# The first x tile of an interleaving kernel as one DMA instead of two halves, and the first y tile issued ahead of the opening barrier

## The chip, the cores and the metric

The kernel runs on one core of a Trainium2 chip. The metric is the device time of one execution in microseconds (us), the median of several runs; a separate, profiled execution gives the profile and the trace.

## The reference

Two float32 arrays x and y of shape 32 x 256 x 1024 are interleaved along their last dimension. Nothing is computed; 67.11 MB are read and 67.11 MB written.

```python
result = np.zeros((batch, seq, dim * 2), dtype=np.float32)
result[..., 0::2] = x
result[..., 1::2] = y
```

## The kernel before

Each input is taken as one flat row of numbers and cut into n = 8 tiles of 128 partitions x 8192 float32 (4 MiB; one partition's row is 32 KiB). On the chip there are two buffers for x tiles (xt), two for y tiles (yt) and two for output (ot). An output buffer is also 128 x 8192, and holds one column half of a tile's result: 4096 numbers of x and 4096 of y per partition, alternating.

Three engines share the work, each with its own program, written out in order:

- SP (SyncE) issues the loads, on one DMA queue (q1 in the profile). For tile k it issues x (line 45) and then y (line 48). From k = 2 on it waits first: for x, until three of the four copies of tile k-2 are done, for y until all four are. The counter for that is the semaphore `woven`, which each copy raises by one.
- DVE (VectorE) makes four copies for each tile: for column half h = 0 and then 1, x into the even places of ot[h] (line 60) and y into its odd places (line 63). Ahead of the first copy it waits for the x tile, ahead of the second for the y tile, and from k = 1 on ahead of each half for the store of the same half of the tile before.
- ACT (ScalarE) issues the stores on a second DMA queue (q10), one of 4 MiB for each half, when that half's two copies are done (lines 67 and 68).

TensorE and GpSimd have no part in the work. The 16 DMA engines of the core serve both queues; a DMA of 128 rows gives each of them 8 rows. In the trace each row is one packet, and each engine ends its share of a DMA with a tiny packet that raises the semaphore.

The first x tile is an exception. Lines 37 and 38 load it as two DMAs, columns 0 to 4095 and 4096 to 8191, so with rows of 16 KiB. The second has a semaphore of its own, `hsem`, and DVE waits for it at line 57, ahead of the second half's x copy. The loop over the loads leaves x out for k = 0 (line 44).

After the program is written, `tile_interleave_kernel` moves two instructions by hand. The opening block of the program holds a barrier over all engines, and on SP a drain ahead of it. The loop of lines 89 to 107 runs twice: each time it takes the first DMA of SP that is still in a later block, and puts it in the opening block just ahead of SP's drain.

```python
for engine in (mybir.EngineType.SP, mybir.EngineType.SP):
    ...
    opening.insert(gate, moved)
```

Before the change, the two that are moved are the halves of the first x tile, and y's first DMA is the first one behind the barrier.

Of the kernel before, what the change touches and what calls it, by code (L numbers as in the profile page):

```python
# [3 lines left out]


def _interleave(nc, x, y, out):
    P = 128
    W = 8192
    H = W // 2  # L10

    total = 1
    for s in x.shape:
        total *= s
    n = total // (P * W)
    assert n * P * W == total

    def rows(ap, names, k):
        flat = ap.rearrange("b s d -> (b s d)")
        return flat[k * names : (k + 1) * names].rearrange("(p w) -> p w", p=P)  # L20

    fp32 = mybir.dt.float32
    xt = [nc.alloc_sbuf_tensor(f"xt{b}", [P, W], fp32).ap() for b in (0, 1)]
    yt = [nc.alloc_sbuf_tensor(f"yt{b}", [P, W], fp32).ap() for b in (0, 1)]
    ot = [nc.alloc_sbuf_tensor(f"ot{b}", [P, W], fp32).ap() for b in (0, 1)]

    xsem = [nc.alloc_semaphore(f"xsem{b}") for b in (0, 1)]
    hsem = nc.alloc_semaphore("hsem")
    ysem = [nc.alloc_semaphore(f"ysem{b}") for b in (0, 1)]
    woven = nc.alloc_semaphore("woven")  # L30
    osem = [nc.alloc_semaphore(f"osem{b}") for b in (0, 1)]

    xs = [rows(x, P * W, k) for k in range(n)]
    ys = [rows(y, P * W, k) for k in range(n)]
    os_ = [rows(out, 2 * P * W, k) for k in range(n)]

    nc.sync.dma_start(out=xt[0][:, :H], in_=xs[0][:, :H]).then_inc(xsem[0], 16)
    nc.sync.dma_start(out=xt[0][:, H:], in_=xs[0][:, H:]).then_inc(hsem, 16)

    for k in range(n):  # L40
        b = k % 2
        if k >= 2:
            nc.sync.wait_ge(woven, 4 * (k - 2) + 3)
        if k:
            nc.sync.dma_start(out=xt[b], in_=xs[k]).then_inc(xsem[b], 16)
        if k >= 2:
            nc.sync.wait_ge(woven, 4 * (k - 2) + 4)
        nc.sync.dma_start(out=yt[b], in_=ys[k]).then_inc(ysem[b], 16)

    for k in range(n):  # L50
        b = k % 2
        for h in (0, 1):
            c = slice(h * H, (h + 1) * H)
            if h == 0:
                nc.vector.wait_ge(xsem[b], 16 * (k // 2 + 1))
            elif k == 0:
                nc.vector.wait_ge(hsem, 16)
            if k:
                nc.vector.wait_ge(osem[h], 16 * k)
            nc.vector.tensor_copy(out=ot[h][:, 0::2], in_=xt[b][:, c]).then_inc(woven, 1)  # L60
            if h == 0:
                nc.vector.wait_ge(ysem[b], 16 * (k // 2 + 1))
            nc.vector.tensor_copy(out=ot[h][:, 1::2], in_=yt[b][:, c]).then_inc(woven, 1)  # L63

    for k in range(n):
        for h in (0, 1):
            nc.scalar.wait_ge(woven, 4 * k + 2 * h + 2)
            nc.scalar.dma_start(
                out=os_[k][:, h * W : (h + 1) * W], in_=ot[h]
            ).then_inc(osem[h], 16)  # L70

    nc.scalar.wait_ge(osem[0], 16 * n)
    used = sorted(s.num for s in [*xsem, hsem, *ysem, woven, osem[0]])
    assert used == list(range(used[0], used[-1] + 1)), used
    nc.scalar.sem_clear(range(used[0], used[-1] + 1))
    nc.sync.nop(nofuse=True).wait_op(osem[1], 16 * n, "sem-ge").then_inc(
        osem[1], -16 * n
    )


def kernel(tc, x, y, out):
    nc = tc.nc
    tc.close()
    tc.compile()

    _interleave(nc, x, y, out)

    blocks = nc.main_func.blocks
    for engine in (mybir.EngineType.SP, mybir.EngineType.SP):
        opening = blocks[0].instructions  # L90
        at, moved = next(
            (b, i)
            for b in blocks[1:]
            for i in b.instructions
            if i.engine == engine and i.opcode == "DMACopy"
        )
        assert not (moved.sync_info and moved.sync_info.on_wait)
        body = at.instructions
        body.remove(moved)
        gate = next(  # L100
            n
            for n, i in enumerate(opening)
            if i.engine == engine and i.opcode == "Drain"
        )
        opening.insert(gate, moved)
        at.instructions = body
        blocks[0].instructions = opening


# [1 line left out]
_INS = ['x', 'y']  # L111
_OUTS = [((32, 256, 2048), 'float32')]


# [23 lines left out]
```

## Time and profile before

| | before |
|---|---|
| median of 3 runs | 314.38 us (314.33 to 314.55) |
| profiled execution | 314.29 us |
| its span, first to last instruction | 313.0 us |
| DVE busy | 72.6 us, 32 copies of 2.29 us |
| moved by DMA | 134.22 MB, mean 429 GB/s |
| load DMAs | 17: two of 2048 KB, fifteen of 4096 KB |
| store DMAs | 16 of 4096 KB |

The span is what the trace covers; the profiled execution's own time is 1.29 us longer. The profile doesn't count the issue of a DMA as busy time, so SP and ACT have no row of their own there; their issues are seen in the timeline as SPq and ACTq. A DMA's time to landing runs from its issue and so holds the time in which it stood in the queue behind others.

### The profile page before, as it was taken

To read this page: it belongs to the slowest core of one execution; us is meant where nothing else is said; L and a number is where in the kernel's file an instruction comes from. 1 tells how busy PE (TensorE), PEld (TensorE's weight loads), DVE (VectorE), ACT (ScalarE), POOL (GpSimd) and SP (SyncE) were. 2 spreads that over 40 slices of the span, in tenths; PEclk is the share of its full clock that TensorE was granted. 3 is DMA by queue.
4 is the path that set the end of the run, shared out by engine and by line. 5 is a ranking of instruction groups with operands and counts; after the bars stand their busy time and mean duration, and the time that the engine had idled before them with its cause. 6 is when DMAs were issued, how large, how long until landed. Compare 5 with 4: busy or idle time off the path is not lost.

```text
span 313.0 us, 113 instructions
## 1 busy us (share of the span) xinstructions
DVE 72.6 (23%) x32; POOL 0.2 (0%) x4
## 2 busy tenths in 40 slices
DVE  0226002231022410325003150031501305013510
POOL 0000000000000000000000000000000000000000
DMA  8999999999999999999999999999999999999998
GB/s 341 463 410 394 469 402 448 423 436 436 419 452 406 465 402 469 402 469 402 469 402 448 423 436 436 419 452 406 465 402 469 402 469 402 465 406 444 427 431 373
DMA packets 4752, 134.22 MB, mean 429 GB/s; under 512 B 528, under 2 KB 528, under 8 KB 528
## 3 DMA queue, kind: packets, MB, share of 16 engines
q1 hardware_dynamic: 2448, 67.11, 50.1%
q10 hardware_dynamic: 2304, 67.11, 49.7%
HBM read 67.11 MB, written 67.11 MB: 429 GB/s over the span
## 4 chain that ended last, share of the span: by engine, by line
DMA 82%; DVE 12%; issue 0%
DMA out_dram<-ot 76%; DVE ot L63 6%; DMA yt<-in_y_dram 6%; DVE ot L60 6%
## 5 line engine op out<-in xcount | busy, mean ns | idle before, releaser
L60 DVE COPY ot<-xt 128x4096 f32<-128x4096 f32 x16 | 36.7, 2295 | 178.8 <-DMA out_dram<-ot 171.5
L63 DVE COPY ot<-yt 128x4096 f32<-128x4096 f32 x16 | 36.7, 2292 | 46.7 <-DMA yt<-in_y_dram 46.7
L122 POOL MEMSET const-bfloat16-1.0<- 128x1 bf16 x1 | 0.1, 101 | 0.0
L122 POOL MEMSET const-uint8-127<- 128x1 uint8 x1 | 0.1, 101 | 0.0
L122 POOL MEMSET const-float32-0.0<- 128x1 f32 x1 | 0.1, 98 | 0.2 <-issue 0.2
L122 POOL MEMSET const-float32-1.0<- 128x1 f32 x1 | 0.1, 98 | 0.0
## 6 DMA issues: line engine op xcount, KB each, us to landing
out_dram<-ot ACTq DMA_DIRECT2D x16, 4096.0 KB, 29.1
yt<-in_y_dram SPq DMA_DIRECT2D x8, 4096.0 KB, 60.8
xt<-in_x_dram SPq DMA_DIRECT2D x7, 4096.0 KB, 43.7
xt<-in_x_dram SPq DMA_DIRECT2D x2, 2048.0 KB, 9.5
```

The lines of the kernel that those rows point to most:

```text
L60: nc.vector.tensor_copy(out=ot[h][:, 0::2], in_=xt[b][:, c]).then_inc(woven, 1)
L63: nc.vector.tensor_copy(out=ot[h][:, 1::2], in_=yt[b][:, c]).then_inc(woven, 1)
L122: nc = _bacc.Bacc("TRN2", target_bir_lowering=False, num_devices=1)
```

## The change

The two half loads and `hsem` go. The first x tile is loaded like every other one, as one DMA of 32 KiB rows on xsem[0], in the loop. The code that moves two of SP's DMAs ahead of the barrier is not touched; the first two are now the first x tile and the first y tile, so y's first DMA goes ahead of the barrier behind x's. DVE's wait for the first x tile now covers the whole tile.

```diff
-    hsem = nc.alloc_semaphore("hsem")
...
-    nc.sync.dma_start(out=xt[0][:, :H], in_=xs[0][:, :H]).then_inc(xsem[0], 16)
-    nc.sync.dma_start(out=xt[0][:, H:], in_=xs[0][:, H:]).then_inc(hsem, 16)
-
     for k in range(n):
         b = k % 2
         if k >= 2:
             nc.sync.wait_ge(woven, 4 * (k - 2) + 3)
-        if k:
-            nc.sync.dma_start(out=xt[b], in_=xs[k]).then_inc(xsem[b], 16)
+        nc.sync.dma_start(out=xt[b], in_=xs[k]).then_inc(xsem[b], 16)
         if k >= 2:
             nc.sync.wait_ge(woven, 4 * (k - 2) + 4)
         nc.sync.dma_start(out=yt[b], in_=ys[k]).then_inc(ysem[b], 16)
...
             if h == 0:
                 nc.vector.wait_ge(xsem[b], 16 * (k // 2 + 1))
-            elif k == 0:
-                nc.vector.wait_ge(hsem, 16)
...
-    used = sorted(s.num for s in [*xsem, hsem, *ysem, woven, osem[0]])
+    used = sorted(s.num for s in [*xsem, *ysem, woven, osem[0]])
```

## The prediction

> **What bounds the kernel now.** I read the page first, for the load of the DMA engines against the chain; then the timeline of the start, where the change lies; then the DMA view in short windows, which gives the mean time of one packet of each size.
>
> The page (each digit is a fortieth of the span, 9 meaning 90% or more; the last two lines are the chain and a queue):
>
> ```profile
> span 313.0 us, 113 instructions
> DVE 72.6 (23%) x32; POOL 0.2 (0%) x4
> DMA  8999999999999999999999999999999999999998
> DMA packets 4752, 134.22 MB, mean 429 GB/s; under 512 B 528, under 2 KB 528, under 8 KB 528
> DMA 82%; DVE 12%; issue 0%
> ```
>
> The chain puts 12% on DVE, as if copies stood in the way of the end. The row of digits says otherwise: in no slice but the first and last do the 16 DMA engines fall below 90%. The windows in the middle (columns: width, DVE busy, POOL busy, clock, DMA share, GB/s) make it exact:
>
> ```profile
> 0.00:1.00 1.00, 0.00 (x0) 0.20 (x4) 1.00 0.00 0
> ...
> 100.00:200.00 100.00, 22.67 (x10) 0.00 (x0) 1.00 1.01 435
> 200.00:290.00 90.00, 22.77 (x10) 0.00 (x0) 1.00 1.00 432
> ```
>
> The share is 1.00 to 1.01 (a packet counts whole where it starts). While DVE copies, the DMA engines work on other tiles. The kernel is a queue of bytes, and its time is what the packets take, plus whatever leaves the queue empty or cold. The start:
>
> ```profile
> 0.00 0.37 SPq L37 DMA_DIRECT2D xt<-in_x_dram  x1
> ...
> 0.42 0.42 SPq L38 DMA_DIRECT2D xt<-in_x_dram  x1
> 1.90 0.33 SPq L48 DMA_DIRECT2D yt<-in_y_dram  x1
> 2.28 0.43 SPq L45 DMA_DIRECT2D xt<-in_x_dram  x1
> 2.76 0.44 SPq L48 DMA_DIRECT2D yt<-in_y_dram  x1
> 7.30 2.30 DVE L60 COPY ot<-xt 128x4096 f32<-128x4096 f32 x1 [7.30 <-DMA xt<-in_x_dram]
> 21.90 2.30 DVE L63 COPY ot<-yt 128x4096 f32<-128x4096 f32 x1 [12.30 <-DMA yt<-in_y_dram]
> ```
>
> SP has put all four first tiles in the queue by 3.2 us. The second half of x lands, by the DMA view, 11.7 us after its issue, at 0.42 + 11.7 = 12.1; y lands at 21.9. DVE has one copy to do at 7.3 and then stands for 12.3 us until y is there.
>
> The DMA view in four windows (1 to 1.5, 4 to 10, 13 to 20, 27.2 to 27.7 us), of each the queue's line: packets, MB, share of 16 engines.
>
> ```profile
> q1 hardware_dynamic: 16, 0.26, 237.5%
> ```
> ```profile
> q1 hardware_dynamic: 175, 2.61, 101.4%
> ```
> ```profile
> q1 hardware_dynamic: 85, 2.79, 92.1%
> ```
> ```profile
> q1 hardware_dynamic: 16, 0.52, 359.5%
> ```
>
> Share times 16 times the window, over the packets, is the time of one. Second line: 1.014 x 16 x 6.0 = 97.3 us, of which 16 tiny completion packets take almost nothing; 97.3 / 159 = 0.612 us for a warm 16 KiB packet. Third: 0.921 x 16 x 7.0 / 85 = 1.213 us for a warm 32 KiB packet. First: 2.375 x 16 x 0.5 / 16 = 1.188 us for the very first packet of each engine, 16 KiB and cold: 0.576 us over a warm one. Fourth: 3.595 x 16 x 0.5 / 16 = 1.798 us for 32 KiB packets just before the first store's packets begin, 0.585 us over a warm one. (Two rounds of packets are slow there; the other, by the same reckoning over 25.7 to 27.7 us, 32 packets at 157.3%, brings the stall to 0.72 us per engine.)
>
> Check of the model, per engine: 248 packets of 32 KiB x 1.213 = 300.8; 16 of 16 KiB x 0.612 = 9.8; 33 completion packets (528 / 16) x 0.009, a duration from the trace's packet records, = 0.3; first packet 1.0 us after the first issue; cold start 0.58; stall at the first store 0.72. Sum 313.2 against a span of 313.0. Nothing of size is missing. The profiled execution is 314.29, so 1.29 lies around the span; the median of 314.38 is 0.09 above it.
>
> **The change, part by part.**
>
> Packets removed: each engine moves 8 rows of the first x tile. Before, 16 packets of 0.612 = 9.79; after, 8 of 1.213 = 9.70. One DMA less is also one completion packet less, 0.01. All of this is on the path, since the engines never rest: -0.09 + -0.01, but the packet times carry a rounding of 0.001 each (16 x 0.001), so I take -0.08. A price for a DMA beyond its packets is rival 2.
>
> SP's issues: L38's 0.42 us goes, and y's first DMA takes its place as the second instruction ahead of SP's drain. The count ahead of the barrier stays at two, so the barrier, which SP reaches last, opens when it did; y is moved past no other DMA on SP, and POOL's queue has none. Behind the barrier x's and y's second DMAs are issued one place earlier, at 1.9 and 2.3. Worth nothing: the engines are busy with x until 12.1, with y until 21.9 and with the second x after that. Were this cover gone (an empty queue at 1.9), y's earlier issue would be worth 1.90 - 0.42 = 1.5 us.
>
> Waits: the wait on the second half goes, and none is added, but DVE's first wait now asks for the whole x tile: 12.1 in place of 7.3. Behind it in DVE's order stand one L60 copy and then L63, which waits for y. 12.1 + 2.3 = 14.4 against 21.9: 7.5 us of cover. Without it the first stores would start up to 2.3 us late, and even then the second x and y tiles (19.4 us of packets) keep the engines busy. The waiters on DVE's counts are ACT (two copies done) and SP (three done), so none hangs on the first copy alone. Cost zero, and the third copy finds its x in place as it does now.
>
> Cold start: the first packet of each engine becomes a 32 KiB one, which the trace of before never starts with. Bounds: the cold part may stay at 0.58 (a wait for first data), or double with the packet to 1.15, +0.58. Below: the trace's packet records show three engines with a short first packet whose second was slow too; folding these into one might save 0.07, and no more can go, as first data must still come. The nearest row is the fourth window: the price of an interruption on 32 KiB packets is 0.585, against 0.576 on 16 KiB ones. It didn't grow with the packet. The packet records also show 7 of the 16 first packets cold by less than 0.54, under the 0.612 that reading a whole packet ahead of writing it would cost. I take 0.
>
> Stall at the first store: 0.72 now, with the same DMAs, waits and copies around it; I take no change.
>
> Sum: 314.29 - 0.08 = 314.21 for a profiled run, 314.38 - 0.08 = 314.30 for the median: 0.03% less. A measurement of this kernel can tell about 0.2%, 0.63 us, from no change.
>
> **The rivals.**
>
> 1. The cold start grows with the packet (slower). Price: +0.58 at the mean; the coldest engine of before took 1.43 us in the packet records, 0.82 over a warm packet, and if that one sets the end, +0.82. With -0.08 this gives 314.88 to 315.12. It decides from a cold part of 1.29 on (0.58 + 0.71), where the total passes +0.63. For it: no row shows a cold 32 KiB load on an empty queue. Against: the fourth window.
>
> 2. Each DMA has a fixed cost, and one DMA fewer saves it (faster). The first half landed at 7.3, its 8 packets take 4.9, so 2.4 us are fixed; saved, the median would be 314.30 - 2.4 = 311.9. Against: the second half landed at 12.1, 4.8 after the first, no more than its own packets. The fixed part is paid once by the start, not by each DMA in a full queue. The Trainium skill, DMA: Bandwidth & Descriptors, section "Anatomy of one DMA — SWDGE (gpsimd) path", gives a fixed cost of about 2.0 us for each DMA, fitted for the other way of issuing; by it the median would be an estimated 312.3. By that rule the halves would land 6.8 us apart, and the trace disagrees with 4.8.
>
> 3. The stall at the first store changes. If the new phase of packets avoids it, 314.30 - 0.72 = 313.58; if it costs twice, 315.02. For: it is the one place after the start that is off the steady pace, and it sits where x's third DMA is issued (26.4 us). Against: what is queued there is the same in kind and order.
>
> 4. The move doesn't take place, and y is issued behind the barrier still: with 10 us of x in the queue, 314.30 all the same.
>
> **How the numbers follow.** Forecast 0.78; rival 1, 0.10; rival 2, 0.02; rival 3, 0.08, half to each side; rival 4, 0.02. Within 0.2%: 0.78 + 0.02 + half of rival 1 (0.05) = 0.85. Slower: 0.05 + 0.04 = 0.09. Faster: 0.04 + 0.02 = 0.06. The forecast alone spans 314.15 (the 0.07, and the runs' own spread of 0.22) to 314.50. The range goes from 314.10 to 314.95, to take in the mean price of rival 1; what is left out is its upper end and rivals 2 and 3, some 0.15.
>
> **What would show it.** Packets fall by 144 to 4608, completion packets to 512. y's issue stands at 0.42, the second x's near 1.9. L60's first copy starts near 12.1 and L63's still near 21.8; if L63 starts at 22.4 or later, rival 1 is at work, and if at 20, rival 2. The window of 1 to 1.5 us should give first packets of 1.21 + 0.58 = 1.79 us each; 2.4 would be rival 1. The slow round near 27.5 us should stay. The prediction is wrong if a slice in mid-span falls below 9, or if the pace of 435 GB/s changes.

## The result, and the profile after

The changed kernel takes 315.18 us (median, 314.53 to 315.68) against 314.48 for the kernel before in the same session (314.33 to 316.05). The ratio is 1.0018, with an interval of 1.001 to 1.0025: some 0.6 us slower, where 314.30 and no change were forecast. The range ended at 314.95, so the result lies above it. Executions of one and the same kernel differ here: of the 20 of the changed kernel, four lie at 314.53 to 314.66 and sixteen at 315.08 and over. The profiled execution is one of the sixteen, 315.17 us.

The page of the profile after, the lines that answer to those of before:

```profile
span 313.8 us, 112 instructions
DVE 72.6 (23%) x32; POOL 0.2 (0%) x4
DMA  9999999999999999999999999999999999999997
DMA packets 4608, 134.22 MB, mean 428 GB/s; under 512 B 512, under 2 KB 512, under 8 KB 512
DMA 83%; DVE 12%; issue 0%; SPq 0%
```

The 144 packets are gone, the DMA engines are as full as before, and the span is 0.8 us longer. The windows of mid-span show the same pace as before:

```profile
100.00:200.00 100.00, 22.67 (x10) 0.00 (x0) 1.00 1.01 435
200.00:290.00 90.00, 22.76 (x10) 0.00 (x0) 1.00 1.00 431
```

The timeline of the start:

```profile
0.41 0.42 SPq L43 DMA_DIRECT2D yt<-in_y_dram  x1
1.89 0.33 SPq L40 DMA_DIRECT2D xt<-in_x_dram  x1
2.27 0.44 SPq L43 DMA_DIRECT2D yt<-in_y_dram  x1
12.20 2.30 DVE L53 COPY ot<-xt 128x4096 f32<-128x4096 f32 x1 [12.20 <-DMA xt<-in_x_dram]
21.91 2.30 DVE L56 COPY ot<-yt 128x4096 f32<-128x4096 f32 x1 [7.41 <-DMA yt<-in_y_dram]
24.12 2.29 DVE L53 COPY ot<-xt 128x4096 f32<-128x4096 f32 x1
24.24 4.76 ACTq L61 DMA_DIRECT2D out_dram<-ot  x2
```

Up to the first store's issue nothing is late: y is there at 21.91 against 21.90, the store goes out at 24.24 against 24.23. The 0.8 us come behind that. The waits (engine, line, what it waited for: us in all, times, longest) say where, first of before and then of after:

```profile
DVE ot L60 <- DMA out_dram<-ot: 171.5, 14, 19.4
```
```profile
DVE ot L53 <- DMA out_dram<-ot: 186.9, 14, 21.4
```

The longest wait for a store, that for the first one's buffer, has grown by 2.0 us. The DMA view around the first store, 25.7 to 30.9 us, first of before and then of after (queue q1 carries the loads, q10 the stores; packets, MB, share):

```profile
q1 hardware_dynamic: 48, 1.57, 83.8%
q10 hardware_dynamic: 16, 0.52, 23.7%
```
```profile
q1 hardware_dynamic: 48, 1.57, 84.4%
q10 hardware_dynamic: 14, 0.46, 20.7%
```

Before, each of the 16 engines starts its first store packet in this window. After, 14 do. The other two are found again at the end, in the DMA view from 312.85 us on, where before has no packet left and after has

```profile
q10 hardware_dynamic: 2, 0.00, 0.1%
```

These are completion packets: two engines finish after the rest, and the DMA is done when the last one is. The trace's packet records show how they came to be late. They don't name the engine, but in a full queue an engine's next packet starts within some nanoseconds of the end of its last one, so each engine's packets can be followed. Here is one ordinary engine of the changed kernel and the two others, as start:duration/queue in ns.

```
24703:1213/1  25912:1340/1  27249:1775/1  29020:1232/10  30249:1213/1   31458:1213/10
24998:1213/1  26207:1213/1  27417:2889/1  30303:1213/1   31512:1213/10
24736:1213/1  25945:1213/1  27155:2359/1  29510:1462/1   30969:1213/10
```

Every engine is slowed while the first store comes in; that is the stall of 0.72 us that the prediction found, and over all engines it is 0.74 us before and 0.77 after by these records. But the two engines lose 1.68 and 1.40 us and start their first store packet one load packet later, behind 23 load packets in place of 22. From then on each packet takes 1.213 again, and nothing is ever caught up: they end at 313.48 and 312.94, all others by 312.55. I call these late engines.

### The profile page after: what moved, and what is told of

The parts are those of the page before. It is cut to its first block, busy times and chain, and to the rows that moved or that the text cites. A ratio compares the mean times of both kernels' runs of the same rounds, so it can differ in the third digit from the quotient of the medians.

```text
span 313.8 us, 112 instructions
## 1 busy us (share of the span) xinstructions
DVE 72.6 (23%) x32; POOL 0.2 (0%) x4
## 2 busy tenths in 40 slices
DMA packets 4608, 134.22 MB, mean 428 GB/s; under 512 B 512, under 2 KB 512, under 8 KB 512
## 4 chain that ended last, share of the span: by engine, by line
DMA 83%; DVE 12%; issue 0%; SPq 0%
DMA out_dram<-ot 76%; DMA yt<-in_y_dram 7%; DVE ot L56 6%; DVE ot L53 6%; SPq L40 0%
```

## The experiments

The share of executions at 315.0 us or over serves as the mark of a late engine in runs without a trace: 3 of 147 for the kernel before, 26 of 31 for the changed kernel. The mark is a coarse one. Two profiled executions below it (tiny_rows16 at 314.86, shift_after at 314.76) also have engines that start their first store one load packet later, and 6 of 11 over the mark is not clearly fewer than 26 of 31. The diffs below show the lines that matter; reserving and clearing an extra semaphore are not shown.

**Which part of the change.** The changed kernel again, beside each part alone.

> The changed kernel unaltered, as the yardstick for the runs beside it. In its trace 14 engines end at 312.2 to 312.6 us and two at 312.9 and 313.5; these two served one more load packet before their first store packet near 29 us. Late-engine theory: most executions lie at 315.1 to 315.4, a few at 314.5 to 314.7 without a late engine, so the median is 0.6 to 0.8 us over before. Cold-start theory (rival 1): every execution is longer by the same 0.5 to 0.8, none near 314.6.

Measured: 1.0023 (1.0014 to 1.0032), 315.19; one execution at 314.47, the other ten from 315.01 to 315.53. Its trace has two late engines, at 313.41 and 313.32. The cold-start theory has no place for the one at 314.47.

```diff
-    for engine in (mybir.EngineType.SP, mybir.EngineType.SP):
+    for engine in (mybir.EngineType.SP,):
```

> The first x tile whole, the first y DMA still behind the barrier. If the 32 KiB rows bring the late engines: most executions at 315.1 to 315.4, as the changed kernel. If y's place ahead of the barrier (and with it the second x and y DMAs 0.4 us earlier) brings them: most at 314.3 to 314.6, as before.

Measured: 1.0022 (1.0013 to 1.0031), 315.13, 6 of 11 at 315.0 or over, the others from 314.68; one late engine in the trace.

```diff
 # in the kernel before, with the first x tile in halves
-    for engine in (mybir.EngineType.SP, mybir.EngineType.SP):
+    for engine in (mybir.EngineType.SP,) * 3:
```

> The first x tile in halves as before, and the first y DMA ahead of the barrier behind them (three DMAs ahead, so the barrier opens some 0.4 us later). If the 32 KiB rows bring the late engines: most executions at 314.3 to 314.6. If y's place does: most at 315.1 to 315.4.

Measured: 0.9997 (0.9988 to 1.0006), 314.38, none of 11 at 315.0 or over. So, by the medians, the whole loss comes with the first x tile in one piece. The other half of the change, y ahead of the barrier, is worth nothing either way, as the prediction said.

**What the stall and the late engines hang on.** A small DMA on the store's queue at the start:

```diff
+    nc.scalar.dma_start(out=ot[1][:, :16], in_=xs[0][:, :16]).then_inc(wsem, 16)
...
+            if k == 0 and h == 1:
+                nc.vector.wait_ge(wsem, 16)
...
-    for engine in (mybir.EngineType.SP, mybir.EngineType.SP):
+    for engine in (mybir.EngineType.SP, mybir.EngineType.SP, mybir.EngineType.Activation):
```

> The changed kernel with one small DMA (128 rows of 64 bytes of x into ot[1], overwritten later) on ACT's queue ahead of the barrier, so that the store queue has been used once before the first store. Cold-queue theory (the slow packets at 25.8 to 29.4 us come from the first use of the second queue): the slow packets go, 0.7 us per engine less, and no engine can be late: 313.7 to 314.1, profile after 24 us all at 1.21 us a packet. Direction theory (they come from the first transfer out of the chip's memory, whichever queue): the slow packets stay, 314.5 to 315.4.

Measured: 1.0002 (0.9994 to 1.0011), 314.51, none of 11 at 315.0 or over. The cold-queue theory falls, since the slow packets stay. The direction theory said that they would, and 314.51 is the lower end of its range; but it had no reason for the late engines to go. The DMA view from 25.7 to 30.9 us of this kernel:

```profile
q1 hardware_dynamic: 48, 1.57, 82.7%
q10 hardware_dynamic: 16, 0.52, 23.6%
```

All 16 engines start their store in time, so the late engines are gone; but the stall stays, 0.67 us per engine in the packet records. Stall and lateness are two things.

The same small DMA written to device memory, so that the first write there is over early:

```diff
+    nc.scalar.dma_start(out=os_[0][:, :16], in_=xs[0][:, :16]).then_inc(wsem, 16)
...
+            if k == 0 and h == 0:
+                nc.scalar.wait_ge(wsem, 16)
```

> The changed kernel with one small DMA on ACT's queue ahead of the barrier, from x in device memory straight to the first 64 bytes of each row of out's first tile (overwritten by the first store, which waits for it). First-store theory (the stall of 0.6 to 0.7 us per engine near 28 us is the price of the first write to device memory): the stall goes, packets between 25 and 30 us take 1.21 to 1.25, and the time is 313.7 to 314.0. Switch theory (the stall comes with the first large packets out of the on-chip buffers, whatever was written before): the stall stays and the time is that of warm_load, 314.4 to 314.6, without late engines.

Measured: 1.0011 (1.0001 to 1.0021), 314.57, 2 of 11 at 315.0 or over, stall 0.70. The first-store theory falls: the stall isn't the price of a first write. The switch theory fits here, but row_halves below has the same first store out of the on-chip buffers and no stall. Late engines are rare, not gone, if the two long executions have one; in the trace (314.93) one engine ends at 313.23, but it lost only 0.77 at the store and was behind from its first packet, at 1.75 us. The warmed queue in the kernel before, with warm_load's edit:

> The kernel before with warm_load's small DMA on ACT's queue. If the warmed store queue and the 16 KiB start cure the same thing (late engines), nothing is left to cure and the time is that of before, 314.3 to 314.5. If warming also saves time of its own, it is below before by 0.1 us or more.

Measured: 1.0002 (0.9993 to 1.0011), 314.42: nothing left to cure. Next, the loads and the second store moved away from the first store, by doing the third copy twice:

```diff
+            if k == 0 and h == 1:
+                nc.vector.tensor_copy(out=ot[h][:, 0::2], in_=xt[b][:, c]).then_inc(dsem, 1)
+                nc.vector.wait_ge(dsem, 1)
             nc.vector.tensor_copy(out=ot[h][:, 0::2], in_=xt[b][:, c]).then_inc(woven, 1)
```

> The changed kernel, with the first tile's third copy (x into ot[1]) done twice, one after the other: x's third DMA, y's third DMA and the second store are issued some 2.4 us later (28.8, 31.0, 31.0 in place of 26.4, 28.6, 28.6); the first store's issue stays at 24.2. If the slow packets and the first store packets hang on the first store's issue: they stay at 25.8 to 29.4. If they hang on x's third load or the second store: the stall, or its end at 29.0, moves by 2.4 us. If late engines come from where x's third DMA falls in the stall: they go, or become more.

Measured: 1.0031 (1.0019 to 1.0043), 315.56. The timeline shows x's load moved from 26.4 to 28.8, and the DMA view from 25.7 to 30.9 shows the same stall in the same place, with 15 engines in time and one late:

```profile
28.77 0.33 SPq L41 DMA_DIRECT2D xt<-in_x_dram  x1
```
```profile
q1 hardware_dynamic: 48, 1.57, 84.8%
q10 hardware_dynamic: 15, 0.49, 22.0%
```

So the stall hangs neither on x's third load nor on the second store. That it follows the first store's own issue is not shown by this, since that issue did not move; shift_before and row_halves below speak against it.

**What it is about the whole x tile.** Halves by partitions in place of columns, two DMAs with 32 KiB rows:

```diff
+    nc.sync.dma_start(out=xt[0][:64], in_=xs[0][:64]).then_inc(xsem[0], 16)
+    nc.sync.dma_start(out=xt[0][64:], in_=xs[0][64:]).then_inc(hsem, 16)
...
+                if k == 0:
+                    nc.vector.wait_ge(hsem, 16)
```

> The first x tile as two DMAs again, but halved by partitions (64 rows of 32 KiB each) and not by columns. Each DMA engine gets 4 + 4 packets of 32 KiB. Packet-size theory (late engines come where the first packets are 32 KiB): as the changed kernel, most at 315.0 to 315.5, one or two engines ending near 313.3. DMA-count theory (two DMAs ahead of y prevent them): as before, 314.3 to 314.6. Count-of-packets theory (more than 14 or so packets per engine on the load queue ahead of the first store prevent them): 10 here in place of 9, so as the changed kernel.

Measured: 1.031 (1.0297 to 1.0324), 324.23, a loss in the load that hides in the time what was looked for. Here are the GB/s of the 40 slices, with the first three at half rate, and x there at 22.85 us, y at 32.47:

```profile
GB/s 195 211 248 451 451 398 451 451 398 451 451 398 451 451 398 451 451 398 451 451 398 451 451 398 451 451 398 451 451 398 451 451 398 451 451 398 451 451 398 386
22.85 2.30 DVE L60 COPY ot<-xt 128x4096 f32<-128x4096 f32 x1 [22.85 <-DMA xt<-in_x_dram]
32.47 2.30 DVE L63 COPY ot<-yt 128x4096 f32<-128x4096 f32 x1 [7.32 <-DMA yt<-in_y_dram]
```

All 16 engines were at work, but a packet took 2.56 us in the records. The Trainium skill, SBUF — State Buffer, section "Door 1: The DMA port swizzle", says that partitions 0 to 63 reach only 8 of 16 ports, and 64 to 127 the other 8; the measured rate, some 213 GB/s between 4 and 20 us, agrees. That the second DMA, for the other half, stood right behind in the queue didn't help.

The trace still answers what was looked for. No engine is late, and there is no stall at all: in the packet records no engine loses more than 0.06 us between 34 and 44 us, though the first store goes out at 34.80 into a full load queue as ever, behind 22 load packets on each engine as in the changed kernel. It lands 23.0 us after its issue, against 23.7 in the kernel before and 25.7 in the changed one. And y lands 10.57 us later than before, while the span of 322.8 is only 9.8 longer. The packet-size and the count theory asked for one or two late engines here; the DMA-count theory asked for none, but tiny_front below has two DMAs ahead of y and late engines. So a first store that joins a full load queue need not cost anything; what spares this kernel, its row halves, the later time of its store or something else, is not shown.

The y tile in column halves, x whole:

```diff
+        if k == 0:
+            nc.sync.dma_start(out=yt[0][:, :H], in_=ys[0][:, :H]).then_inc(ysem[0], 16)
+            nc.sync.dma_start(out=yt[0][:, H:], in_=ys[0][:, H:]).then_inc(hsem, 16)
...
+                if k == 0:
+                    nc.vector.wait_ge(hsem, 16)
```

> The first x tile whole, the first y tile in two column halves of 16 KiB rows. First-packet theory (it is the size of the very first, cold packets that matters): as the changed kernel, most at 315.0 to 315.5. Count-of-packets theory (or 16 KiB packets anywhere ahead of the first store): as before, 314.3 to 314.6.

Measured: 1.0013 (1.0004 to 1.0021), 314.86, 5 of 12 at 315.0 or over: half cured, with no late engine in the trace (314.50); it fits neither theory. One DMA with rows of two pieces:

```diff
+        two = lambda t: t.rearrange("p (a w) -> p a w", a=2) if k == 0 else t
+        nc.sync.dma_start(out=two(xt[b]), in_=two(xs[k])).then_inc(xsem[b], 16)
```

> The first x tile as one DMA whose rows are written as two pieces of 16 KiB; if the pieces stay apart, the trace shows 16 packets of 16 KiB per engine from one DMA. Packet-size theory: 314.3 to 314.6, as before. DMA-count theory: 315.0 to 315.5, as the changed kernel. If the pieces are merged again into 32 KiB packets, it is the changed kernel once more.

Measured: 1.0027 (1.0016 to 1.0038), 315.29. The trace has 4608 packets, none of 16 KiB, so the pieces were merged and this is the changed kernel once more; 5 of 6 at 315.0 or over. Its profiled execution, at 315.70, shows that the start varies too between executions of the same packets:

```profile
22.32 2.30 DVE L57 COPY ot<-yt 128x4096 f32<-128x4096 f32 x1 [7.39 <-DMA yt<-in_y_dram]
```

That is 0.41 later than in the changed kernel's trace. One engine's first packet began at 2.14 us there, where the last one of the changed kernel began at 1.73.

The halving moved to the second x tile:

```diff
+        if k == 1:
+            nc.sync.dma_start(out=xt[1][:, :H], in_=xs[1][:, :H]).then_inc(xsem[1], 16)
+            nc.sync.dma_start(out=xt[1][:, H:], in_=xs[1][:, H:]).then_inc(hsem, 16)
...
+            if k == 1 and h == 1:
+                nc.vector.wait_ge(hsem, 16)
```

> The changed kernel with the second x tile (k = 1), and not the first, in two column halves, so that the packets under way when the first store comes are 16 KiB. If an engine is late by one load packet that it takes first, it is late by 0.6 us and not 1.2: executions with late engines at 314.6 to 314.9, the others at 314.3 to 314.5. Start theory: how often engines are late doesn't change. Count theory: late engines go, 314.3 to 314.6 throughout.

Measured: 1.0028 (1.0017 to 1.0039), 315.27, all 7 at 315.0 or over. With 16 KiB load packets under way when the store comes in, the stall itself grew, to a mean of 1.13 us per engine (0.7 to 1.9). Not all of the lost time lies there: 14 of the 16 engines also stand without a packet for up to 0.7 us in all near 293 us, when the loads are done and the next store has not begun. That a late engine loses one load packet's time, and half of it with 16 KiB, falls; how many engines were late for the other reason can't be told from it.

A small load ahead of the second x tile (tiny_mid), with 16 rows only (tiny_rows16), twice (tiny_twice), and ahead of the first x tile (tiny_front, where three DMAs of SP go ahead of the barrier):

```diff
 # tiny_mid
         nc.sync.dma_start(out=yt[b], in_=ys[k]).then_inc(ysem[b], 16)
+        if k == 0:
+            nc.sync.dma_start(out=ot[1][:, :16], in_=xs[0][:, :16]).then_inc(wsem, 16)
 # tiny_rows16, in its place
+            nc.sync.dma_start(out=ot[1][:16, :16], in_=xs[0][:16, :16]).then_inc(wsem, 16)
 # tiny_twice, in its place
+            for j in (0, 1):
+                nc.sync.dma_start(out=ot[1][:, 16 * j : 16 * j + 16], in_=xs[0][:, 16 * j : 16 * j + 16]).then_inc(wsem, 16)
 # tiny_front: tiny_mid's DMA ahead of the loop over the loads
+    nc.sync.dma_start(out=ot[1][:, :16], in_=xs[0][:, :16]).then_inc(wsem, 16)
...
 # in all four, ahead of the third copy (32 in tiny_twice)
+            if k == 0 and h == 1:
+                nc.vector.wait_ge(wsem, 16)
```

> The changed kernel with one small load (128 rows of 64 bytes into ot[1], overwritten later) on SP's queue behind the second x and y tiles' place in the first round: after y's first DMA and behind the barrier. The start is that of the changed kernel; ahead of the first store the load queue has held 9 more packets per engine, as many as halving a tile adds. Count theory: no late engines, 314.3 to 314.6. Start theory (the 32 KiB packets at the cold start): as the changed kernel, most at 315.0 to 315.5.

> tiny_mid with 16 rows in place of 128: one small packet and one completion packet per engine, so 2 more packets ahead of the first store in place of 9; the second x tile is issued at 2.3 as in tiny_mid. Count theory: nearly the changed kernel, most at 315.0 to 315.5. Issue-time theory, and DMA-count theory: none late, 314.3 to 314.6.

> tiny_mid with two small loads, 18 more packets per engine; the second x tile is issued near 2.7. If more packets are enough: 314.3 to 314.7. If it is a position in a ring that counts (late engines come back at other counts): 315.0 to 315.5. Issue-time theory: none late.

> The small load of tiny_mid put ahead of the first x tile, as the very first DMA; three DMAs ahead of the barrier. The cold packets are 64 bytes long. Cold-start theory (rival 1): the first 32 KiB packet is no longer cold, the y tile lands near 21.9 + 0.1, no more. Count theory for the late engines: none late, 314.3 to 314.7.

| kernel | ratio (interval) | median | at 315.0 or over |
|---|---|---|---|
| tiny_mid | 1.0004 (0.9995 to 1.0013) | 314.53 | 1 of 11 |
| tiny_rows16 | 1.0022 (1.0013 to 1.0031) | 315.05 | 6 of 11 |
| tiny_twice | 1.0004 (0.9995 to 1.0013) | 314.65 | 0 of 11 |
| tiny_front | 1.0034 (1.0021 to 1.0046) | 315.55 | 5 of 5 |

After tiny_mid the count of packets looked like the cause: the start is that of the changed kernel, and nine more packets per engine cure it. tiny_twice, with 18, has no execution over 315.0 either, though its stall is 0.85 per engine and its last engine ends at 313.00. tiny_rows16, with two, hardly helps: 6 of 11, a median of 315.05, and five engines in its trace start their store one load packet later. But tiny_front has the same nine packets, ahead of x, and is over 315.0 in every execution. Its y lands 0.41 late, at 22.32, so the mark counts for less there; but two engines are late in its trace, with 1.44 and 1.76 us lost at the store. So a count alone isn't it. The second x tile issued later, with no packet added:

```diff
+        if k == 1:
+            nc.sync.wait_ge(xsem[0], 16)
         nc.sync.dma_start(out=xt[b], in_=xs[k]).then_inc(xsem[b], 16)
```

> The changed kernel, but SP issues the second x and y tiles only when the first x tile has landed (12.2 us in place of 1.9; the queue still holds y for 9.7 us). Same packets, later issue. Count theory: late engines as in the changed kernel, most executions at 315.0 to 315.5. Issue-time theory (an issue at 1.9 while the engines start cold makes engines late): none, 314.3 to 314.6.

Measured: 1.0012 (1.0003 to 1.0021), 314.82, 5 of 11 at 315.0 or over, and three engines late in its trace: not the issue time alone either.

Last, the first store moved by half a packet, in both kernels:

```diff
                 nc.vector.wait_ge(ysem[b], 16 * (k // 2 + 1))
+                if k == 0:
+                    nc.vector.tensor_copy(out=ot[1][:, :1024], in_=xt[0][:, :1024]).then_inc(dsem, 1)
...
 # ahead of the third copy
+            if k == 0 and h == 1:
+                nc.vector.wait_ge(dsem, 1)
```

> The changed kernel with one small copy more on DVE (128 x 1024, into ot[1], overwritten later) between y's landing and the second copy, so that the first store is issued some 0.6 us later, half a packet. Phase theory: the share of late executions changes much, to nearly none or to all, and the late engines are others. Start theory (the start of the kernel fixes which engines are late): most executions at 315.0 to 315.5 as in the changed kernel.

> The same small copy in the kernel before: first store 0.6 us later. Phase theory: late engines appear in a good share of executions, 315.0 and over. Start theory: 314.3 to 314.6, as before.

Measured: the changed kernel 1.0019 (1.001 to 1.0027), 315.0, 6 of 11; the kernel before 1.0001 (0.9992 to 1.001), 314.53, 1 of 11. The phase theory asked for late engines in the kernel before, and there are none to speak of. What was loaded ahead weighs more than where in a packet the store falls.

The two traces say more. In shift_before the first store goes out at 24.86 in place of 24.23. Its issue, and the DMA view from 25.7 to 30.9 us:

```profile
24.86 4.76 ACTq L73 DMA_DIRECT2D out_dram<-ot  x2
```
```profile
q1 hardware_dynamic: 48, 1.57, 84.7%
q10 hardware_dynamic: 16, 0.52, 23.5%
```

This is nearly the view of the kernel before (83.8% and 23.7%). The slow packets lie where they did, and the store's first packets begin at 29.12 to 29.48, where they began at 29.06 to 29.40. So the stall did not move with the store's issue. In shift_after ten of the 16 engines start the store one load packet later, but lose only 0.66 to 1.06 us each. One load packet more is not in itself the large loss of a late engine.

**What is settled and what is open.** Settled: the loss comes with the first x tile in one piece, it is paid while the first store comes in, and an execution is long because a few of the 16 engines (one to three in most of these traces) lose some 0.6 to 1.1 us more than the rest there and keep it to the end. Halving the first x tile, a small load ahead of the second one, or a first use of the store's queue at the start each remove it or nearly so. Open is what an engine does in these extra microseconds, why the stall is there at all when row_halves has none, and what the cures have in common; the number of packets, the time of issue, the first write and the phase were each tried and none explains all. One lead is left: in the seven traces with one to three late engines (those of the changed kernel, x_whole_y_behind, one_dma_16k, late_h1, wait_x0 and tiny_front), 9 of the 13 late engines are among the four of the 16 whose first packet began last. That the start decides who is late is suggested by this, not shown. No kernel tried beats the one before by more than its interval.

## Why the prediction was right or wrong

- **What bounds the kernel.** Right: the DMA engines are full, the pace in mid-span is unchanged, and the 0.8 us are lost in one place.
- **Packets removed.** The count is right (4608). The gain of 0.08 us can't be seen: y lands at 21.91 against 21.90, as the cold start took it back.
- **SP's issues, barrier and waits.** Right to the place: y at 0.41, second x at 1.89, first copy at 12.20, and halves_y_ahead at 0.9997 confirms the zero.
- **Cold start.** Taken at no change. The window from 1 to 1.5 us has 13 packets at

```profile
q1 hardware_dynamic: 13, 0.43, 312.0%
```

so 3.120 x 16 x 0.5 / 13 = 1.92 us each, 0.71 over a warm one in place of 0.58. That is 0.13 more, within the bounds that were given, and it leaves y at 21.91 where 21.8 was forecast. (The window holds 13 of the 16 first packets. Over the first 15 us the packet records give 0.70 us per engine against 0.65 before.) Rival 1, which asked for 22.4, falls. Its price of 315.12 came near the result for a wrong reason. The 22.32 of one_dma_16k isn't rival 1 either: there a packet began late, and it was no longer than the others.
- **Stall at the first store.** This is the step that failed: "0.72 now, with the same DMAs, waits and copies around it; I take no change". The mean hardly changed (0.74 to 0.77), but the sum was made per engine from means, and the end is set by the slowest of 16 engines. In the trace of before no engine lost more than 0.88 us there, so mean and maximum lay close; in the changed kernel one lost 1.68 and ended 0.9 us after the last engine of before. Rival 3 had the place, with 0.04 for the slower side and 315.02 for its price, and its argument against, that what is queued there is the same, is what the runs disproved: a difference 25 us earlier, in what the load queue had carried, decided it.
- **Rivals 2 and 4.** Neither: nothing near 311.9 was seen, and y did move ahead.
- **The range.** It left out the slower half of rival 3. With a stall known to sit on the path and not understood, its doubling in a single engine (0.9 us) belonged inside.

## What to carry to other kernels

In a kernel bound by DMA, sum the time for the slowest of the 16 engines, not for their mean: a loss of 1 us in one engine is a loss of 1 us in the kernel if the queues never run dry, since no other engine takes over its rows. Compare the number of completion packets in the last microsecond of two traces; two stragglers among 16 don't show in busy shares or GB/s. And where one execution in a profile stands for several kinds of execution, look at the list of times before reading the trace as the kernel.

## What the runs showed of the hardware that was not expected

- When the first store joins a full load queue, the engines lose 0.65 to 0.94 us on average in all kernels here but two, once; in the kernel before this lies between 25.8 and 29.4 us. It isn't the queue's first use (warm_load, 0.67) nor the first write (warm_store, 0.70). With 16 KiB load packets it was 1.13 (x1_halves), and in row_halves, whose first store goes out at 34.80, it was not there (0.06 at most).
- A store issued into busy engines begins its first packet 3.9 us (row_halves) to 4.8 us (the kernel before) after its issue, where the first load on idle engines begins 1.0 us after.
- A load into 64 partitions runs at half rate (2.56 us for a 32 KiB packet in place of 1.213), also when the other 64 follow at once in the same queue: y lands 10.57 us later for 4 MiB.
- The two queues alternate packet by packet on each engine while both have work, whatever the size: in warm_load's records one 64-byte packet of the second queue, 0.011 us long, follows each 32 KiB one of the first from its second on.
